# One tile's gate table summed in DRAM by accumulating indirect DMAs, its gathers given seven buffers and a higher priority

## The chip, the cores and the metric

The kernel runs on one core of a Trainium2 chip. The metric is the device time of one execution in microseconds. The kernel before took 2860.1 us (median of 3 runs, 2859.8 to 2860.92). Engines are named as in the profile: PE (matrix products), DVE, ACT and POOL (vector work), SP (issues most DMAs; indirect DMAs are issued by POOL).

## The reference, cut to what matters

One layer over 1024 rows (tokens) of width 1024: token mixing (convolutions and a gated spatial product), then a mixer called PEER, then a small gated embedding and a norm. PEER picks, for each row and each of 8 heads, 16 of 16384 experts and sums their one-neuron outputs:

```python
s1 = jnp.einsum("thd,hkd->thk", q1, sub_keys[:, 0])    # 128 scores per head and side
v1, i1 = lax.top_k(s1, TOPK)                           # the same for s2
vals, ci = lax.top_k(cand, TOPK)                       # 16 best of the 16 x 16 sums
idx = (e1 * N_KEYS + e2).reshape(t, PEER_HEADS * TOPK) # 128 picks per row
gates = jax.nn.softmax(vals, axis=-1)
ug = expert_u[ib]
act = jax.nn.gelu(jnp.einsum("td,tkd->tk", xb, ug)) * gb
vg = expert_v[ib]
return jnp.einsum("tk,tkd->td", act, vg)
```

The 16 picks of one head of a row are different experts; picks of different heads may be the same one, and then their weights add up.

## The kernel before

The 1024 rows are eight tiles of 128. PEER is done in three ways. For tiles 1 to 4 (`DENSE`) every expert is computed with matrix products against the whole of `expert_uT` and `expert_v`, and a table `Wd[t]` in DRAM (16384 experts by 128 rows, zero where nothing is picked) gives each product its gate. For tiles 5 to 7 (`GATHER`) the picked rows of `expert_u` and `expert_v` are fetched by indirect DMAs, 128 rows of 4 KB per DMA, and multiplied on DVE. Tile 0 (`MIXED`) takes one half of each: its rows of `expert_u` are gathered, which gives the 128 activations of a row times their gates (`weights[0]`, tile `wm`), and these go as values into a table `Wd[0]`, with which the dense products of `expert_v` are weighted.

The program has three stages. The **front** treats the tiles in pairs (0,1), (2,3), (4,5), (6,7): `mix_in` (projections, convolution taps on DVE), `mix_out` (output projection, norm; POOL computes the reciprocal root `rB`), `choose` (query products, the top-16 searches on DVE, `select`). A pair's `finish`, which holds its `choose`, is issued after the next pair's `mix_in`. Beside them run the gate tables: `gate_table(t)` is a generator that `fill()` advances a step at a time. It goes through the tile's 128 rows in quads of four: DVE writes a one-hot of the first key for the quad (`oh1`, L415), another engine a one-hot of the second key times the gate (`oh2`: POOL for every odd quad, L421; for even quads ACT in two steps, L426 and L427, or DVE for tile 0, L423), PE multiplies them (L430), and ACT copies the product into the tile `st` (L431). Eight quads fill `st`, which SP stores with one 2 MB DMA (L434); four such stores make a table. The gathers of tile 0 (`u_step(MIXED, ...)`, L536, and their products on DVE, L538) are written in the code after the last pair's `choose`, in four blocks of 32, each followed by a gelu on ACT (L546) and the product with the gates on POOL (L547); tile 0's table is the last of the fillers. One block of tile 5's gathers ends the front. The **dense** stage runs over the 128 blocks of experts, with the gathers of tiles 5 to 7 beside it, and then the **back** finishes all tiles.

The order in which instructions stand on each engine is set when the program is built, by a scheduler that simulates time and takes ready instructions by priority (the place in the code, unless `high_priority` moves it up). On the chip each engine runs its list in that order: an instruction that waits holds back all that stand behind it on its engine, and SP's list does the same for DMAs. So a gather that is late in the code can stand early in POOL's list. A pool with `bufs=n` gives a tile name n buffers in turn; the next writer of a buffer waits for the last reader of it. `g` (a gathered tile) has 3 buffers in the front (`FG`), `st` 2.

Of the kernel before, what the change touches and what calls it, by code (L numbers as in the profile page):

```python
# [8 lines left out]
F32 = mybir.dt.float32  # L9
# [5 lines left out]
OP = mybir.AluOpType  # L15
AX = mybir.AxisListType
P = 128
D = 1024
# [8 lines left out]
def trunk(ctx: ExitStack, tc: tile.TileContext, x, pT, w_inF, w_inV, chan, ln_c, w_sT, b_s, w_out, g_row,  # L27
# [30 lines left out]

    UAT, GAT, RATE = 6, 6, 3

    FG, BG = 3, 5

# [12 lines left out]
    TG = 32  # L75
    Wd = {t: dram.tile([P, P // TG, P, TG], F32, name=f"Wd{t}") for t in TABLE}

    fctx = ExitStack()
# [60 lines left out]
    def mix_in(t0, nt):  # L139
# [23 lines left out]
        for j in range(3):  # L163
            pg, pv = zchunks(3 + j, j)
            sg = work.tile([P, T], F32, name="sg")
            nc.scalar.activation(sg, pg, AF.Sigmoid)
            ya = work.tile([P, 30 + T], F32, name="ya", bufs=3)
            nc.scalar.copy(ya[:, 0:30], halo_a[:, j])
            nc.vector.tensor_mul(ya[:, 30:], pv, sg)
            nc.scalar.copy(halo_a[:, j], ya[:, T:T + 30])  # L170
            yas.append(ya)
        for j in range(3):
# [10 lines left out]
        for j in range(2):  # L183
# [12 lines left out]
            pb, = zchunks(6 + j)  # L196
            nc.vector.tensor_mul(yT[:, 3 + j], pb, acc)


        vn = group.tile([P, nt, 384], F32, name="vn")  # L200
        for s in range(3):
            wv = wstream.tile([P, 8, P], F32, name="w1", bufs=2)
            nc.sync.dma_start(wv, w_inV[s])
            for t in range(nt):
                pv = psum.tile([P, 2, 64], F32, name="z")
                for c in range(8):
                    nc.tensor.matmul(pv, aT[:, c, t * P:(t + 1) * P], wv[:, c], start=c == 0, stop=c == 7)
                nc.scalar.copy(vn[:, t, s * P:s * P + P], pv.rearrange("p h c -> p (h c)"))
        for t in range(nt):
            st = small.tile([P, 4, 6], F32, name="st")  # L210
# [105 lines left out]

    filler, n_gt = [], [0]

    def fill():

        for _ in range(RATE):
            while filler:
                if next(filler[0], None) is None:
                    filler.pop(0)
                    continue
                break
# [9 lines left out]
    def select(t, tv, ti):  # L336
# [27 lines left out]
        own = work if t in GATHER else wbp  # L364
        e = own.tile([P, 2, NH * K], F32, name="e", bufs=2 if t in GATHER else 5)
        for side in range(2):
# [28 lines left out]
    def gate_table(t):  # L395
# [12 lines left out]
        for g in range(P // TG):  # L408
            st = wbp.tile([P, P, TG], F32, name="st")
            for q in range(0, TG, 4):  # L410
                c = g * TG + q
                n_gt[0] += 1

                oh1 = wbp.tile([P, 4, P], F32, name="oh1", bufs=2)
# [3 lines left out]
                for k in range(4):  # L418
                    k2, gk = eT[:, 1, c + k:c + k + 1], gT[:, c + k:c + k + 1]
                    if n_gt[0] % 2:  # L420
# [11 lines left out]
                if q % 8:  # L432
                    yield True
            nc.sync.dma_start(Wd[t][:, g], st)  # L434

    def dense():
# [87 lines left out]
    def u_step(t, b, front=False):  # L524
# [9 lines left out]
        for k in range(b * KB, (b + 1) * KB):  # L534
            ug = gath.tile([P, D], F32, name="g")
            nc.gpsimd.indirect_dma_start(out=ug, out_offset=None, in_=expert_u,  # L536
                                         in_offset=bass.IndirectOffsetOnAxis(ap=idx[:, k:k + 1], axis=0))
            nc.vector.scalar_tensor_tensor(ug, ug, 1.0, ns[t, front], op0=OP.mult, op1=OP.mult,  # L538
                                           accum_out=dots[:, k - b * KB:k - b * KB + 1])
        if t == MIXED:  # L540
# [9 lines left out]
    def experts(tiles):  # L550
# [26 lines left out]
        for st in steps:  # L577
            if st not in acts:
                u_step(*st)
            if prev is not None:  # L580
# [18 lines left out]
    def back_out(t, h, nT):  # L599
# [26 lines left out]
        nc.sync.dma_start(out[t * P:(t + 1) * P], o_)  # L626

    def finish(t0, nt, nT):
# [16 lines left out]
    finish(*waits.pop())  # L645
    while filler:
        fill()
    for b in range(UE):
        u_step(GATHER[0], b, True)
    fctx.close()  # L650
# [94 lines left out]
```

## Time and profile before

| | |
|---|---|
| median of 3 runs | 2860.1 us |
| the profiled execution | 2848.63 us, span 2846.6 us |
| busy share of the span | PE 92%, DVE 76%, POOL 69%, ACT 35% |
| front: start to the first dense product (PE L481) | 0 to 1085 us |
| dense stage | to about 2620 us |
| back | to 2846.6 us |

A trace tells for each engine which instruction ran when, and which other one it waited for before. A busy share over the whole span says little here, since the three stages have different limits; the view by stretches gives the shares apart.

### The profile page before, as it was taken

Reading aid. Unit: us, or ns where it says so; the run is one execution under the profiler, and the core shown is the slowest. Engines: PE = TensorE matmul, PEld = TensorE weight load, DVE = VectorE, ACT = ScalarE, POOL = GpSimd, SP = SyncE. Lnnn points to the kernel's source line nnn. Section 1 sums busy time; section 2 is a strip of 40 time slices with the busy share of each in tenths; the row PEclk is TensorE's granted clock in tenths of the full one; section 3 lists DMA queues with packets and bytes.
Section 4 is the critical chain, followed back from the end, with each engine's and each line's share of the span. In section 5 each row is a group of like instructions: output and inputs, shape, how many; then the busy total and the mean of one; then the engine's idle time right before and its main releaser. Section 6 shows DMA issues by size and latency. Waiting matters only on the chain.

```text
span 2846.6 us, 37627 instructions
## 1 busy us (share of the span) xinstructions
PE 2607.7 (92%) x12671; PEld 2197.8 (77%) x12671; DVE 2163.0 (76%) x4738; ACT 1007.2 (35%) x1930; POOL 1951.6 (69%) x1740
## 2 busy tenths in 40 slices
PE   7999989798768568999999999999999999999988
PEld 6888878787767556888787888878788787888777
DVE  5566998899977886777777777776777777777776
ACT  3324237345655534232322223222232322222352
POOL 0000067368776787887888878887887878888783
PEclk9999999899778779999999999999999999999999
DMA  6354577787757559999999999999999999999885
GB/s 209 121 194 146 190 269 275 283 299 268 236 210 268 207 211 337 329 338 334 330 346 326 336 343 344 337 332 335 335 335 325 332 351 323 341 337 328 312 290 174
DMA packets 299697, 820.92 MB, mean 288 GB/s; under 512 B 26096, under 2 KB 117616, under 8 KB 296944
## 3 DMA queue, kind: packets, MB, share of 16 engines
q0 software_dynamic: 129024, 469.82, 45.9%
q1 hardware_dynamic: 170480, 348.70, 36.0%
q8 instruction: 100, 1.64, 0.2%
q14 instruction: 93, 0.76, 0.1%
HBM read 764.93 MB, written 53.48 MB: 288 GB/s over the span
## 4 chain that ended last, share of the span: by engine, by line
PE 43%; DVE 18%; DMA 18%; POOL 11%; issue 8%; ACT 1%; SPq 0%; POOLq 0%; DVEq 0%; ACTq 0%
DMA g<-expert_u,idx 8%; DMA g<-expert_v,idx 7%; PE mm L504 5%; PE mm L505 5%; PE mm L506 5%; PE z L481 5%; PE z L482 5%; PE z L483 5%; DVE g L538 4%; POOL g L536 3%; PE z L158 3%; PE mm L612 3%; POOL oh L421 3%; POOL vl L477 3%; PE mm L299 2%
## 5 line engine op out<-in xcount | busy, mean ns | idle before, releaser
L536 POOL DMA_INDIRECT g<-expert_u,idx x512 | 509.5, 995 | 340.1 <-DVE g L538 137.1
L568 DVE SCALAR_TENSOR_TENSOR accP<-g,act,accP 128x1024 f32<-128x1024 f32 x384 | 493.6, 1285 | 205.3 <-DMA g<-expert_v,idx 199.9
L538 DVE SCALAR_TENSOR_TENSOR g<-g,nP 128x1024 f32<-128x1024 f32 x352 | 423.2, 1215 | 168.9 <-DMA g<-expert_u,idx 167.7
L566 POOL DMA_INDIRECT g<-expert_v,idx x384 | 367.2, 956 | 143.4 <-DVE accP L568 62.0
L504 PE MATMUL mm<-vh,ah 128*128 128x512 f32 x1024 | 399.8, 392 | 16.1 <-DVE accA L508 8.8
L481 PE MATMUL z<-nh,uh 128*128 128x512 f32 x1024 | 401.5, 392 | 8.1 <-DVE al L490 5.9
L482 PE MATMUL z<-nl,uh 128*128 128x512 f32 x1024 | 400.2, 391 | 1.6 <-DVE nl L446 1.5
L483 PE MATMUL z<-nh,ul 128*128 128x512 f32 x1024 | 399.8, 390 | 0.0
L505 PE MATMUL mm<-vl,ah 128*128 128x512 f32 x1024 | 398.7, 390 | 0.0
L506 PE MATMUL mm<-vh,al 128*128 128x512 f32 x1024 | 396.4, 390 | 0.0
L421 POOL TENSOR_SCALAR oh<-iota,eT,gT 128x128 f32<-128x128 f32 x320 | 325.2, 1024 | 43.7 <-PE gt L430 39.0
L430 PE MATMUL gt<-oh,oh 128*128 128x128 f32 x1280 | 228.0, 327 | 131.6 <-DVE oh L415 69.7
L468 ACT CAST uh<-u 128x1024 fp32r<-128x1024 f32 x128 | 134.7, 1052 | 566.9 <-PE z L482 449.5
L477 POOL TENSOR_TENSOR vl<-v,vh 128x512 fp32r<-128x512 f32 x256 | 327.5, 1300 | 2.6
L430 PEld LDWEIGHTS gt<-oh,oh 128*128 128x128 f32 x1280 | 199.5, 229 | 160.7 <-POOL oh L421 92.1
L470 POOL TENSOR_TENSOR ul<-u,uh 128x1024 fp32r<-128x1024 f32 x128 | 308.7, 2412 | 3.9 <-ACT uh L468 1.9
L475 ACT CAST vh<-v 128x512 fp32r<-128x512 f32 x256 | 153.7, 621 | 319.1 <-DMA v<-expert_v 266.6
L538 DVE SCALAR_TENSOR_TENSOR g<-g,hrow 128x1024 f32<-128x1024 f32 x160 | 196.4, 1230 | 74.5 <-DMA g<-expert_u,idx 74.3
L299 PE MATMUL mm<-nT,w 128*128 128x256 f32 x1024 | 243.1, 387 | 0.0
L504 PEld LDWEIGHTS mm<-vh,ah 128*128 128x128 f32 x1024 | 193.0, 189 | 59.3 <-DVE accA L508 11.8
L508 DVE TENSOR_TENSOR accA<-mm,accA 128x512 f32<-128x512 f32 x320 | 218.1, 685 | 26.2 <-PE mm L506 25.6
L481 PEld LDWEIGHTS z<-nh,uh 128*128 128x128 f32 x1024 | 193.6, 189 | 53.0 <-DVE al L490 10.6
(367 smaller groups left out, 4593.6 us busy)
## 6 DMA issues: line engine op xcount, KB each, us to landing
u<-expert_uT SPq DMA_DIRECT2D x128, 512.0 KB, 6.1
v<-expert_v SPq DMA_DIRECT2D x128, 512.0 KB, 5.0
Wd<-st SPq DMA_DIRECT2D x20, 2048.0 KB, 8.9
w<-w_q SPq DMA_DIRECT2D x64, 512.0 KB, 4.5
w<-Wd SPq DMA_DIRECT2D x128, 256.0 KB, 10.2
w<-w_inF SPq DMA_DIRECT2D x60, 512.0 KB, 4.1
wo<-w_out SPq DMA_DIRECT2D x32, 512.0 KB, 3.4
g<-expert_u,idx POOLq DMA_INDIRECT x512, 6.2
```

Of the source, the lines that this page charges most:

```text
L421: nc.gpsimd.tensor_scalar(oh2[:, k], iota, k2, gk, op0=OP.is_equal, op1=OP.mult)
L430: nc.tensor.matmul(pw[:, :, k], oh2[:, k], oh1[:, k], start=True, stop=True)
L477: nc.gpsimd.tensor_tensor(vl, v[:, s * 512:s * 512 + 512], vh.bitcast(F32), op=OP.subtract)
L481: nc.tensor.matmul(ph, uh[:, c], nh[:, c], start=c == 0, stop=False)
L482: nc.tensor.matmul(ph, uh[:, c], nl[:, c], start=False, stop=False)
L483: nc.tensor.matmul(ph, ul[:, c], nh[:, c], start=False, stop=c == 7)
L504: nc.tensor.matmul(po, ah[:, c], vh, start=i == 0, stop=False)
L505: nc.tensor.matmul(po, ah[:, c], vl, start=False, stop=False)
L506: nc.tensor.matmul(po, al[:, c], vh, start=False, stop=i == NG - 1)
L536: nc.gpsimd.indirect_dma_start(out=ug, out_offset=None, in_=expert_u, in_offset=bass.IndirectOffsetOnAxis(ap=idx[:, k:k + 1], axis=0))
L538: nc.vector.scalar_tensor_tensor(ug, ug, 1.0, ns[t, front], op0=OP.mult, op1=OP.mult, accum_out=dots[:, k - b * KB:k - b * KB + 1])
L568: nc.vector.scalar_tensor_tensor(acc, vg, act[:, k:k + 1], acc, op0=OP.mult, op1=OP.add)
```

## The change

Tile 0's work is taken out of the chain of code that follows the last `choose`, and its table is no longer made of one-hots.

- `finish` hands tile 0, as soon as its picks are there, to a new list `slow`: the generator `mixed` runs the four blocks of gathers and then `add_table`. `fill()` advances `slow` by 14 steps (`STEP`), and is also called in `mix_in` at eight places. Each gather and its product are issued with `high_priority(offset=1000)`. `FG` goes from 3 to 7 buffers.
- `add_table` issues 128 indirect DMAs from POOL, one per pick: each adds 128 numbers of 4 bytes (the weights of pick k of the 128 rows) into `Wd[0]` at 128 computed places. The adds of one head are declared independent of each other; the head's last one waits for the other 15, and the next head's adds wait for it.
- The four parts of `Wd[0]` are first zeroed: POOL clears a tile `zero` (it is the first holder of `st`'s buffer), and SP stores it four times, 2 MB each.
- `add_places` computes the places: two DVE instructions on 128 x 128 values.
- `st` goes from 2 buffers to 1, the keys `e` of tiles 0 to 4 from 5 to 3.
- The one-hot branch on DVE (L423) goes, since only tile 0 used it. The other four tables stay as they were.

```diff
+    AHEAD, PM, PR = 1000, 2, (1,)
+    RATE, STEP = 3, 14
-    FG, BG = 3, 5
+    FG, BG = 7, 5
...
+        for _ in range(STEP):
+            turn[0] += 1
+            for w in slow[turn[0] % 2:2] + slow[:turn[0] % 2]:
+                if next(w, None) is None:
+                    slow.remove(w)
...
-            st = wbp.tile([P, P, TG], F32, name="st")
+            st = wbp.tile([P, P, TG], F32, name="st", bufs=1)
...
-                    elif t == MIXED:
-                        nc.vector.tensor_scalar(oh2[:, k], iotaP, k2, gk, op0=OP.is_equal, op1=OP.mult)
...
+    def add_table(t, at):
+        gate = weights.get(t, picks[t][1])
+        flat = Wd[t].rearrange("p g e t -> (p g e t)")[:, None]
+        last = None
+        for h in range(NH):
+            adds = []
+            for k in range(h * K, h * K + K):
+                i = nc.gpsimd.indirect_dma_start(out=flat,
+                                                 out_offset=bass.IndirectOffsetOnAxis(ap=at[:, k:k + 1], axis=0),
+                                                 in_=gate[:, k:k + 1], in_offset=None, compute_op=OP.add)
+                i = getattr(i, "ins", i)
+                if len(adds) < K - 1:
+                    for j in adds:
+                        tc.declare_no_dep(i, j, reason="picks of one head are different experts")
+                    if adds and last is not None:
+                        tc.add_manual_dep(i, last.name, SYNC, reason="picks of different heads may be the same")
+                else:
+                    for j in adds:
+                        tc.add_manual_dep(i, j.name, SYNC, reason="the head's last add ends all of them")
+                adds.append(i)
+                yield True
+            last = i
+
+    def mixed(t, at):
+        for b in range(P // KB):
+            yield from u_step(t, b, True)
+        yield from add_table(t, at)
...
+            with tc.high_priority(offset=AHEAD if t == MIXED else 0):
+                ug = gath.tile([P, D], F32, name="g")
...
+    zero = wbp.tile([P, P, TG], F32, name="st", bufs=1)
+    nc.gpsimd.memset(zero, 0.0)
+    for t in ADDED:
+        for g in range(P // TG):
+            nc.sync.dma_start(Wd[t][:, g], zero)
...
     def finish(t0, nt, nT):
         choose(t0, nt, nT)
-        if t0 == UAT:
-            for b in range(P // KB):
-                u_step(MIXED, b, True)
-        filler.extend(gate_table(t0 + t) for t in range(nt) if t0 + t in DENSE)
-        if t0 == GAT:
-            filler.append(gate_table(MIXED))
+        for t in range(t0, t0 + nt):
+            if t in ADDED:
+                slow.append((mixed if t == MIXED else add_table)(t, add_places(t)))
+            elif t in DENSE:
+                filler.append(gate_table(t))
```

The order of the instructions shows three places. The first is SP's list at the very start of the program; `w_...<-w_inF` are the weights of `mix_in`'s products, `w<-w_q` the query weights. Before:

```order
L260 DMA h<-x 128x2x1024
L263 DMA wo<-w_out 128x1024 x2
L294 DMA sk<-skT 128x256
L297 DMA w_1372<-w_q 128x1024
L297 DMA w_1382<-w_q 128x1024
L294 DMA sk<-skT 128x256
L145 DMA a<-x 128x1024 x2
L156 DMA w_227<-w_inF 128x1024
L156 DMA w_237<-w_inF 128x1024
```

and now:

```order
L268 DMA h<-x 128x2x1024
L271 DMA wo<-w_out 128x1024 x2
L693 DMA Wd_96<-st 128x4096 x4
L302 DMA sk<-skT 128x256
L305 DMA w_1383<-w_q 128x1024
L305 DMA w_1393<-w_q 128x1024
L302 DMA sk<-skT 128x256
L150 DMA a<-x 128x1024 x2
L161 DMA w_238<-w_inF 128x1024
```

The four zeroing stores stand ahead of the third weight tile of `mix_in` (`w_227`, now `w_238`) and of two query weight tiles.

The second is POOL's list around the two `rB` of the last pair (tiles 6 and 7), which `mix_out` needs before that pair's queries can start. `oh` is a quad's one-hots (four instructions), `g` a gather, `Wd_96<-wm,at` an add, `wm<-wm,gate` the end of a block of tile 0. Before:

```order
L421 TENSOR_SCALAR oh_4811<-iota,eT,gT 128x128 x4
L536 DMA g<-expert_u,idx 128x1024 x2
L421 TENSOR_SCALAR oh_5452<-iota,eT,gT 128x128 x4
L536 DMA g<-expert_u,idx 128x1024
L421 TENSOR_SCALAR oh_5482<-iota,eT,gT 128x128 x4
L536 DMA g<-expert_u,idx 128x1024 x2
L122 TENSOR_TENSOR rB<-ss_6972,half 128x1
L122 TENSOR_TENSOR rB<-ss_6991,half 128x1
L421 TENSOR_SCALAR oh_5512<-iota,eT,gT 128x128 x4
L421 TENSOR_SCALAR oh_5598<-iota,eT,gT 128x128 x4
```

and now:

```order
L602 TENSOR_TENSOR wm<-wm,gate 128x32
L467 DMA Wd_96<-wm,at 2097152x1 x15
L437 TENSOR_SCALAR oh_4869<-iota,eT,gT 128x128 x4
L467 DMA Wd_96<-wm,at 2097152x1
L437 TENSOR_SCALAR oh_4899<-iota,eT,gT 128x128 x4
L467 DMA Wd_96<-wm,at 2097152x1 x15
L437 TENSOR_SCALAR oh_4951<-iota,eT,gT 128x128 x4
L127 TENSOR_TENSOR rB<-ss_7516,half 128x1
L127 TENSOR_TENSOR rB<-ss_7535,half 128x1
L467 DMA Wd_96<-wm,at 2097152x1
L437 TENSOR_SCALAR oh_4981<-iota,eT,gT 128x128 x4
L437 TENSOR_SCALAR oh_5011<-iota,eT,gT 128x128 x4
```

Before, 118 gathers and 168 one-hots stand ahead of this pair of `rB`; now 128 gathers, 116 one-hots and 127 adds do.

The third is ACT's list in the last table (tile 0's before, tile 4's now), where `st<-gt` copies a quad's product. Before:

```order
L431 COPY st<-gt 128x128x4 x2
L371 CAST tb<-ti 128x1024
L431 COPY st<-gt 128x128x4 x2
L371 CAST tb<-ti 128x1024
L431 COPY st<-gt 128x128x4 x4
L371 CAST tb<-ti 128x1024
L431 COPY st<-gt 128x128x4 x18
L530 ACTIVATE nP<-hrow,rB 128x1024
```

and now:

```order
L439 ACTIVATE oh_7296<-iota,eT 128x128 x4
L440 ACTIVATE oh_7296<-oh_7296,gT,mT 128x128 x2
L444 COPY st<-gt 128x128x4
L440 ACTIVATE oh_7296<-oh_7296,gT,mT 128x128 x2
L444 COPY st<-gt 128x128x4
L439 ACTIVATE oh_7348<-iota,eT 128x128 x4
L440 ACTIVATE oh_7348<-oh_7348,gT,mT 128x128 x4
L439 ACTIVATE oh_7378<-iota,eT 128x128 x4
L440 ACTIVATE oh_7378<-oh_7378,gT,mT 128x128 x4
L444 COPY st<-gt 128x128x4 x4
```

Before, the copies follow one another, 18 in a row at the end; now ACT makes the one-hots of every second quad too, and between the last copy of one `st` and the first of the next (which waits for the store of the first) stand two sets of one-hots. On PE, 50 of 160 quads stand behind the last query product before, 39 of 128 now.

## Rows read from the trace of the kernel before

**Rows 1.** stretches of the kernel: busy time of each engine, granted clock, DMA share
```profile
core 0: us, PE busy (x) PEld busy (x) DVE busy (x) ACT busy (x) POOL busy (x), PEclk, DMA share, GB/s
0.00:348.00 348.00, 319.28 (x1865) 282.94 (x1866) 235.86 (x833) 111.09 (x233) 15.91 (x24) 0.99 0.50 167
348.00:547.00 199.00, 171.65 (x1084) 157.05 (x1083) 172.61 (x635) 99.42 (x240) 125.33 (x120) 0.93 0.80 280
547.00:810.00 263.00, 215.88 (x1307) 193.92 (x1306) 246.16 (x808) 143.79 (x343) 187.19 (x177) 0.90 0.76 267
810.00:944.00 134.00, 108.62 (x569) 96.01 (x569) 99.65 (x348) 71.39 (x170) 93.68 (x87) 0.85 0.63 222
944.00:1083.00 139.00, 83.28 (x399) 68.93 (x397) 113.58 (x388) 62.93 (x132) 116.34 (x119) 0.74 0.61 225
1083.00:2620.00 1537.00, 1506.53 (x6567) 1235.20 (x6568) 1129.07 (x1535) 434.70 (x676) 1263.11 (x1058) 0.99 0.95 336
```

**Rows 2.** chain that ended last, 20 to 35 us: start, length, what
```profile
20.12 3.73 PE z L158 x16
23.88 3.99 DMA w<-w_inF
27.91 7.19 PE z L158 x32
```

**Rows 3.** DVE, 348 to 810 us: its waits for gathers (total, times, longest)
```profile
DVE g L538 <- DMA g<-expert_u,idx: 43.0, 22, 6.4
```

**Rows 4.** DVE, 810 to 944 us: its waits for gathers
```profile
DVE g L538 <- DMA g<-expert_u,idx: 21.6, 7, 5.5
```

**Rows 5.** SP queue in order of time, near 11 us
```profile
10.79 0.43 SPq L294 DMA_DIRECT2D sk<-skT  x1
```

**Rows 6.** stretches between 20 and 30 us (columns as in Rows 1)
```profile
20.00:25.00 5.00, 4.88 (x23) 4.31 (x24) 0.00 (x0) 1.10 (x5) 0.00 (x0) 1.00 1.03 400
25.00:30.00 5.00, 4.39 (x21) 3.55 (x20) 0.73 (x3) 4.57 (x7) 1.00 (x2) 1.00 0.66 230
```

**Rows 7.** tile st: its four-per-table stores, from issue to landing
```profile
DMA to landing us min/median/max: 6.7/8.9/10.6
```

**Rows 8.** POOL in order of time: start, length, what, idle before
```profile
348.10 1.37 POOL L536 DMA_INDIRECT g<-expert_u,idx  x1 [16.84 <-DVE idx L392]
349.77 1.51 POOL L536 DMA_INDIRECT g<-expert_u,idx  x1 [0.30 <-issue]
357.23 0.95 POOL L536 DMA_INDIRECT g<-expert_u,idx  x1 [4.62 <-DVE g L538]
408.61 1.03 POOL L536 DMA_INDIRECT g<-expert_u,idx  x1 [0.17 <-issue]
809.50 1.77 POOL L122 TENSOR_TENSOR rB<-ss,half 128x1 f32<-128x1 f32 x2
```

**Rows 9.** POOL by line up to 1092 us: busy, mean ns, idle before
```profile
L421 POOL TENSOR_SCALAR oh<-iota,eT,gT 128x128 f32<-128x128 f32 x320 | 325.2, 1024 | 43.7 <-PE gt L430 39.0 <-ACT eT L407 1.8 <-DVE oh L377 0.6
L536 POOL DMA_INDIRECT g<-expert_u,idx x168 | 184.9, 1100 | 186.6 <-DVE g L538 87.2 <-DVE idx L392 16.8 <-DVE tv L333 13.9
```

**Rows 10.** DVE by line up to 1092 us
```profile
L538 DVE SCALAR_TENSOR_TENSOR g<-g,hrow 128x1024 f32<-128x1024 f32 x160 | 196.4, 1230 | 74.5 <-DMA g<-expert_u,idx 74.3
L415 DVE TENSOR_TENSOR oh<-iotaP,eT 128x512 f32<-128x512 f32 x160 | 106.8, 677 | 18.1 <-PE gt L430 18.1
L423 DVE TENSOR_SCALAR oh<-iotaP,eT,gT 128x128 f32<-128x128 f32 x64 | 21.9, 399 | 0.0
```

**Rows 11.** DMA issues, 348 to 810 us: the gathers, median us to landing
```profile
g<-expert_u,idx POOLq DMA_INDIRECT x118, 5.9
```

**Rows 12.** ACT by line up to 1092 us
```profile
L426 ACT ACTIVATE oh<-iota,eT 128x128 f32<-128x128 f32 x256 | 81.9, 396 | 0.0
L427 ACT ACTIVATE oh<-oh,gT,mT 128x128 f32<-128x128 f32 x256 | 107.9, 486 | 0.0
L431 ACT COPY st<-gt 128x512 f32<-128x512 f32 x160 | 91.6, 585 | 212.4 <-PE gt L430 211.7
```

More of the change, by code (lines that the diff above doesn't have):

```diff
@@ L16 @@
 AX = mybir.AxisListType
+SYNC = mybir.DependencyInfo(mybir.DependencyClass.Sync, mybir.DependencyReason.DATA)
 P = 128
@@ L76, in trunk @@
     Wd = {t: dram.tile([P, P // TG, P, TG], F32, name=f"Wd{t}") for t in TABLE}
+    ADDED = (0,)
     fctx = ExitStack()
@@ L171, in mix_in @@
             yas.append(ya)
+            fill()
         for j in range(3):
@@ L197, in mix_in @@
             nc.vector.tensor_mul(yT[:, 3 + j], pb, acc)
+            fill()
         vn = group.tile([P, nt, 384], F32, name="vn")
@@ L208, in mix_in @@
                 nc.scalar.copy(vn[:, t, s * P:s * P + P], pv.rearrange("p h c -> p (h c)"))
+            fill()
         for t in range(nt):
@@ L315, in choose @@
             picks[t0 + t] = select(t0 + t, *top[t])
-    filler, n_gt = [], [0]
+    filler, slow, turn, n_gt = [], [], [0], [0]
     def fill():
@@ L324, in fill @@
                     filler.pop(0)
+                    continue
+                break
+        for _ in range(STEP):
[3 more added lines that the diff above has]
+                    slow.remove(w)
                     continue
@@ L364, in select @@
         own = work if t in GATHER else wbp
-        e = own.tile([P, 2, NH * K], F32, name="e", bufs=2 if t in GATHER else 5)
+        e = own.tile([P, 2, NH * K], F32, name="e", bufs=2 if t in GATHER else 3)
         for side in range(2):
@@ L434, in gate_table, with add_places @@
             nc.sync.dma_start(Wd[t][:, g], st)
+    def add_places(t):
+        e = keys[t]
+        at = wbp.tile([P, NH * K], I32, name="at", bufs=3)
+        row = wbp.tile([P, NH * K], F32, name="row", bufs=1)
+        nc.vector.tensor_scalar(row, e[:, 0], float(TG), place, op0=OP.mult, op1=OP.add)
+        nc.vector.scalar_tensor_tensor(at, e[:, 1], float(P * P), row, op0=OP.mult, op1=OP.add)
+        return at
+    def add_table(t, at):
[24 more added lines that the diff above has]
+        yield from add_table(t, at)
     def dense():
@@ L534, in u_step @@
         for k in range(b * KB, (b + 1) * KB):
[L535 to L539, printed above, removed]
+            with tc.high_priority(offset=AHEAD if t == MIXED else 0):
+                ug = gath.tile([P, D], F32, name="g")
+                nc.gpsimd.indirect_dma_start(out=ug, out_offset=None, in_=expert_u,
+                                             in_offset=bass.IndirectOffsetOnAxis(ap=idx[:, k:k + 1], axis=0))
+                nc.vector.scalar_tensor_tensor(ug, ug, 1.0, ns[t, front], op0=OP.mult, op1=OP.mult,
+                                               accum_out=dots[:, k - b * KB:k - b * KB + 1])
+            yield True
         if t == MIXED:
@@ L578, in experts @@
             if st not in acts:
-                u_step(*st)
+                for _ in u_step(*st):
+                    pass
             if prev is not None:
@@ L626, in back_out @@
         nc.sync.dma_start(out[t * P:(t + 1) * P], o_)
+    place = fconst.tile([P, 1], F32, name="place")
+    for g in range(P // TG):
+        nc.gpsimd.iota(place[g * TG:g * TG + TG], pattern=[[0, 1]], base=g * P * TG, channel_multiplier=1,
+                       allow_small_or_imprecise_dtypes=True)
+    zero = wbp.tile([P, P, TG], F32, name="st", bufs=1)
+    nc.gpsimd.memset(zero, 0.0)
+    for t in ADDED:
+        for g in range(P // TG):
+            nc.sync.dma_start(Wd[t][:, g], zero)
     def finish(t0, nt, nT):
         choose(t0, nt, nT)
-        if t0 == UAT:
-            for b in range(P // KB):
-                u_step(MIXED, b, True)
-        filler.extend(gate_table(t0 + t) for t in range(nt) if t0 + t in DENSE)
-        if t0 == GAT:
-            filler.append(gate_table(MIXED))
+        for t in range(t0, t0 + nt):
[3 more added lines that the diff above has]
+                filler.append(gate_table(t))
     waits = []
@@ L645, in trunk @@
     finish(*waits.pop())
-    while filler:
+    while filler or slow:
         fill()
     for b in range(UE):
-        u_step(GATHER[0], b, True)
+        for _ in u_step(GATHER[0], b, True):
+            pass
     fctx.close()
```

3 lines of the change are left out of this document (1 added, 2 removed).

## Prediction

> **What bounds the kernel now.** I read the stretches first [rows 1]. From 1083 us on TensorE is busy 1506.5 of 1537 us, and this stage keeps its code and its order; only its start can move. So the question is when the last of the four tables lies in DRAM. Before that the limits differ by stretch. Up to 348 us it is TensorE (319.3 of 348); the chain of waits runs there through products and the weight tiles that they wait for [rows 2]. From 348 to 810, the gathers of tile 0 beside the one-hots, DVE is the fullest: 172.6 + 246.2 = 418.8 of 462 us, and the missing 43 us are its waits for gathers, 43.0 us in 22 waits [rows 3]; POOL has 125.3 + 187.2 = 312.5. From 810 to 944, with the last pair's queries, no engine is full and DVE waits 21.6 us for gathers [rows 4]. From 944 to 1083 the rest of the tables is made: POOL 116.3, DVE 113.6 of 139 us. The lists in order of time I read for what stands around POOL's gathers.
>
> **The change part by part. Zeroing.** The four stores of 128 x 4096 numbers, 8.39 MB together, stand in SP's list where `sk` is issued at 10.79 us [rows 5]; POOL's clearing of the tile has nothing ahead of it. Behind them stands the third weight tile of `mix_in`, and that tile is on the chain: it was issued at 23.88, took 3.99, and the products start at 27.91 when it lands [rows 2]. The DMA engines are full there, share 1.03 at 400 GB/s from 20 to 25 us and still 0.66 from 25 to 30 [rows 6]. With 8.39 MB put ahead, the tile lands 8.39 MB / 400 GB/s = 21 us later. TensorE is the limit up to 348 us, so this reaches the first picks: 348 becomes 369. Bounds: 0, if the weights pass beside the stores; 26.8, four times the shortest landing (6.7 us) of a store of this shape [rows 7], one after another. I take 21, which rests on the rate measured at that place.
>
> **348 to the last pair's `rB` (809.5 us, [rows 8]).** POOL gains the adds. Its list up to `rB`: 128 gathers x 1.100 = 141; 116 one-hots x 1.024 = 119 [rows 9]; other work as before, 312.5 - 118 x 1.100 - 168 x 1.024 = 11; and 127 adds. No add is in the trace of before. The nearest row is a gather, which takes as many places (128) from a column and writes other descriptors from them: 127 x 1.10 = 140. Between DMA instructions there is a pause of 0.17 to 0.30 us with nothing to wait for [rows 8]; 255 x 0.2 = 51. Sum 141 + 119 + 11 + 140 + 51 = 462 us. DVE's own list up to the same place gains 13 products and loses 24 batched one-hots: 13 x 1.23 = +16 and 24 x 0.68 = -16 [rows 10], so DVE keeps 419. For one add with its pause the low bound is 0.30 (the pause alone, the work hidden), the high one 2.5 (twice 1.10 and 0.3, as numbers are added and not only written); I take 1.30, as the undisturbed gather shows 0.95 and 1.03 + 0.17 and the mean is 1.10.
>
> The Trainium skill (DMA: Bandwidth & Descriptors, Anatomy of one DMA — SWDGE path) calls the writing of descriptors a small, variable part of such a DMA. The row says that POOL is held about 1 us by 128 of them, so here the measurement decides; by the page alone the adds would cost about their pauses, and the front would come out near case A below.
>
> POOL's 462 take the place of DVE's 419 as the limit, and waits come on top. The adds of a head wait for the head before, and the head's last add for the other 15; behind a waiting add stand the next gathers, one-hots and the `rB`, all on POOL. For most heads 8 to 10 one-hots (8 to 10 us) stand between an add and the one that waits for it; for the last two only a quad's four (4 x 1.02 = 4.1 us). A landing takes 5.9 us as a gather does [rows 11], so two waits of 1.8 = 4 us are left. Adds can't start before the first block of 32 gathers and products is done; until then POOL has 39 gathers and 24 one-hots, 39 x 1.30 + 24 x 1.02 = 75 us, and runs into DVE, which does the picks and products: I put 15 us for that, worked out from the 16.84 and 4.62 us that POOL waits for DVE around its first gathers [rows 8] with the seven buffers taking off some of it (an estimate, 0 to 30). The seven buffers hide most of DVE's 43 us; a third, 16 us, I leave as coupling of the two engines. Waits: 4 + 15 + 16 = 35. `rB` at 369 + 462 + 35 = 866 instead of 809.5.
>
> The skill's same page and section gives a fixed completion of about 2.0 us for such a DMA; the row shows 5.9 at this load. By the page the two waits at the end go, and `rB` stands 4 us earlier.
>
> **`rB` to the last query product.** 134 us before; the 21.6 us of gather waits [rows 4] end, since the gathers stand far ahead, but the table work between the queries stays; I count 12 of them: 122, so 988.
>
> **The end of the tables.** Behind the last query product 39 quads stand instead of 50, and they are tile 4's, of which ACT makes the one-hots of every second. For eight quads (one `st`) ACT has 4 sets of 4 x (81.9 + 107.9) / 256 = 2.97 us, 11.9, and 8 copies of 91.6 / 160 = 0.57, 4.6 [rows 12]: 16.4 us. `st` has one buffer now: the first copy of the next one waits until the store has landed, 8.9 us in the median [rows 7] and 0.3 to issue, of which ACT covers two sets, 5.9: 3.3 us more, 19.7. 39 / 8 x 19.7 = 96. ACT's other work there, 62.9 [rows 1] - 50 x 0.57 - 9 sets x 2.97 (tile 4's 18 quads) = 7.6, and one set of POOL's, 4.1, ahead of the first copy: 12. So 108 instead of 139. POOL has 19 or 20 quads x 4 x 1.02 = 80 there and DVE less than before (35 batched one-hots x 0.68 = 24 and the picks), neither the limit. ACT becomes it; before it mainly waited for TensorE's `gt` (211.7 us over all copies, [rows 12]).
>
> **Sum.** 866 + 122 + 108 = 1096 instead of 1083: 13 us later. The profiled execution took 2848.63 us in all with a span of 2846.6, so 2861.6. The median of the three timed runs, 2860.1, lies 11.5 above the profiled one, so the forecast is 2873 us.
>
> **Rivals.**
> A: POOL is not the limit. If an add and its pause cost 0.3 to 0.9 us, or the gathers with seven buffers keep DVE full all the time, DVE's 419 count: 369 + 419 + 18 of waits = 806, and 806 + 122 + 108 = 1036, 47 us earlier: 2813. For it: DVE waits 43.0 us for gathers now, POOL is idle for a third. Against it: 1.10 us for each gather. The point that decides: 1083 - 122 - 108 - 369 = 484 us; is POOL's work with its waits under this, the kernel is faster, above it slower. My 497 lies 13 above, and 0.1 us less for each add would do it.
> B: the adds land slowly. Each reads and writes 128 numbers of 4 bytes in DRAM, which no row shows; the nearest slow landing is the `st` store, 10.6 us at most [rows 7]. Then the last two heads wait 2 x 6.5 and the others up to 2 x 1 to 2 each: some 29 us more, 2902. At 20 us, 12 waits of 11 and three of 16 = 180: 3040. I give the far one little.
> C: the zeroing lies beside other loads, since the engines have room after 30 us: 21 us back, 2852. Against: share 1.03 just there.
> D: the change moves little. Tile 0's gathers stood from the first picks on before as well (the first at 348.10, 118 of 128 ahead of the last `rB`), so little waits went that weren't covered; table work saved and zeroing cancel: 2860.
>
> **Chances.** The forecast (POOL full, 2855 to 2905) 0.46, A with the faster half of C 0.33, B 0.12, D and what lies near it 0.09. A measurement of this kernel can tell some 0.2%, 5.7 us. Faster by more: A, and 0.03 of the forecast's and D's lower edge, 0.36. Within: 0.16, from D and the forecast's lower part. Slower: 0.48. The range takes in A's 2813 and the near case of B up to adds of 1.5 us with waits: 2810 to 2935.
>
> **What would show it.** In the profile of the changed kernel: the third `w_inF` landing near 49 us and the first gather near 369 (right), near 28 and 348 (C). POOL busy over nine tenths from 400 to 866 us and the adds' mean near 1.1 us with few waits (right); below 0.8 (A); POOL idle behind adds of landing time over 10 us (B). DVE's waits for gathers near zero; `rB` of the last pair near 866; the last query product near 988; ACT waiting for the stores of `st` some 3 us each and the last table store issued near 1096. The forecast is wrong if POOL is idle for a fourth of the stretch from 400 us on while DVE is full, or if the first products don't wait for the zeroing.

## The result and the profile after

The changed kernel takes 3009.78 us (median of four runs, 2997.45 to 3014.78) against 2860.47 us: ratio 1.0513, 95% interval 1.0485 to 1.0542, some 149 us slower. Forecast were 2873 us and a range up to 2935; the sign was right, the size was not. The profiled execution took 2997.45 us with a span of 2995.4.

The stretches of the kernel after, cut at the same events as in [rows 1]: first gather, last pair's `rB`, last query product, first dense product (columns as there).

```profile
0.00:375.00 375.00, 323.68 (x1857) 285.58 (x1858) 239.16 (x833) 111.01 (x232) 19.86 (x29) 0.95 0.51 176
375.00:976.00 601.00, 394.01 (x2199) 349.86 (x2197) 429.89 (x1461) 202.73 (x457) 506.29 (x383) 0.81 0.68 210
976.00:1114.00 138.00, 114.37 (x585) 98.31 (x585) 99.42 (x340) 75.10 (x186) 108.10 (x102) 0.86 0.65 239
1114.00:1227.00 113.00, 68.61 (x319) 59.21 (x318) 74.62 (x289) 88.60 (x216) 75.84 (x80) 0.68 0.50 181
1227.00:2765.00 1538.00, 1506.50 (x6587) 1235.27 (x6587) 1124.30 (x1526) 433.59 (x672) 1266.57 (x1058) 1.00 0.95 335
```

The three stretches in the middle for the kernel before:

```profile
348.00:811.00 463.00, 388.53 (x2393) 351.98 (x2392) 419.77 (x1445) 243.33 (x582) 313.48 (x297) 0.91 0.78 272
811.00:941.00 130.00, 105.57 (x551) 93.34 (x550) 95.65 (x337) 70.69 (x169) 89.89 (x84) 0.85 0.64 225
941.00:1085.00 144.00, 85.33 (x413) 70.61 (x411) 117.14 (x396) 65.52 (x136) 119.18 (x121) 0.75 0.61 224
```

The dense stage is as long as it was (1538 us, before 1537). In the front +27 to the first picks, +138 from there to `rB`, +8 over the queries, -31 at the end of the tables: +142. In the second stretch DVE is no longer the fullest engine (430 of 601, before 420 of 463); POOL is, 506 of 601.

POOL by line in that stretch of the kernel after (busy, mean ns, idle before and what ended it):

```profile
L467 POOL DMA_INDIRECT Wd<-wm,at x127 | 210.6, 1658 | 41.0 <-issue 34.4 <-DMA Wd<-wm,at 5.1 <-POOL wm L602 1.0
L590 POOL DMA_INDIRECT g<-expert_u,idx x128 | 149.3, 1167 | 62.0 <-issue 18.3 <-DVE idx L407 17.7 <-DVE g L592 7.8
L437 POOL TENSOR_SCALAR oh<-iota,eT,gT 128x128 f32<-128x128 f32 x116 | 141.0, 1306 | 3.0 <-PE gt L443 0.9 <-ACT eT L422 0.7
```

An add holds POOL 1.66 us in the mean and 0.32 us pass ahead of it: 252 us for 127. Only 5.1 us of that are waits for other adds to land, and they land in 3.6 us in the median. The gathers' 62.0 us include the 17.7 ahead of the first of them. POOL is busy 506.3 us and in a pause without a wait for another 34.4 + 18.3: 559 of 601 us, so its list is full.

What that does to the others is read from the waits, TensorE's of before and of after (from the first gather to `rB`; total, times, longest), and DVE's of after, which answer to [rows 3]:

```profile
PE gt L430 <- DVE oh L415: 31.5, 11, 8.5
PE gt L430 <- POOL oh L421: 13.6, 13, 3.9
```

```profile
PE gt L443 <- POOL oh L437: 163.6, 32, 26.5
```

```profile
DVE g L592 <- DMA g<-expert_u,idx: 118.0, 42, 15.9
```

The profile names the gathers' DMA as what DVE waits for, 118.0 us with seven buffers. But a gather lands in 5.6 us in the median, before in 5.9 [rows 11]; it is issued late, since it stands behind adds in POOL's list. TensorE takes its list in order, so a quad's product that waits for one-hots holds up the queries behind it. One such place, first POOL and then TensorE in order of time:

```profile
508.27 1.54 POOL L467 DMA_INDIRECT Wd<-wm,at  x1 [0.30 <-issue]
510.12 1.54 POOL L467 DMA_INDIRECT Wd<-wm,at  x1 [0.31 <-issue]
511.97 1.03 POOL L590 DMA_INDIRECT g<-expert_u,idx  x1 [0.30 <-issue]
513.30 0.96 POOL L590 DMA_INDIRECT g<-expert_u,idx  x1 [0.30 <-DMA Wd<-wm,at]
514.56 1.60 POOL L467 DMA_INDIRECT Wd<-wm,at  x1 [0.30 <-issue]
515.64 2.46 POOL L437 TENSOR_SCALAR oh<-iota,eT,gT 128x128 f32<-128x128 f32 x1
```

```profile
518.15 2.08 PE L443 MATMUL gt<-oh,oh 128*128 128x128 f32 x8 [16.51 <-POOL oh L437]
```

Fourteen adds in a row, 484.20 to 511.66, 1.54 us each for the shortest; the two gathers behind them take 1.03 and 0.96. TensorE waits 16.51 us for the one-hots behind them.

The zeroing is seen on the chain at the start, which answers to [rows 2]:

```profile
13.28 22.18 DMA Wd<-st
...
35.53 12.18 DMA w<-w_inF
...
47.75 9.56 PE z L163 x32
```

The products that began at 27.91 now begin at 47.75, and the first gather at 375.42 instead of 348.10.

### The profile page after: what moved, and what is told of

It is laid out like the page before. It is cut to its first block, busy times and chain, and to the rows that moved or that the text cites. A ratio compares the mean times of both kernels' runs of the same rounds, so it can differ in the third digit from the quotient of the medians.

```text
span 2995.4 us, 37011 instructions
## 1 busy us (share of the span) xinstructions
PE 2609.7 (87%) x12412; PEld 2192.3 (73%) x12412; DVE 2133.3 (71%) x4644; ACT 993.3 (33%) x1897; POOL 2124.5 (71%) x1809
## 4 chain that ended last, share of the span: by engine, by line
PE 40%; DMA 19%; POOL 17%; DVE 12%; issue 9%; ACT 2%; SPq 0%; POOLq 0%; DVEq 0%; ACTq 0%
DMA g<-expert_v,idx 7%; DMA g<-expert_u,idx 7%; POOL Wd L467 5%; PE mm L557 5%; PE mm L559 5%; PE mm L558 5%; PE z L534 4%; PE z L535 4%; PE z L536 4%; PE z L163 4%; POOL g L590 4%; POOL oh L437 3%; DVE g L592 3%; PE mm L307 2%; PE mm L668 2%
## 5 line engine op out<-in xcount | busy, mean ns | idle before, releaser
L590 POOL DMA_INDIRECT g<-expert_u,idx x512 | 519.2, 1014 | 200.6 <-issue 80.5
L443 PE MATMUL gt<-oh,oh 128*128 128x128 f32 x1024 | 208.3, 356 | 236.8 <-POOL oh L437 183.9
L443 PEld LDWEIGHTS gt<-oh,oh 128*128 128x128 f32 x1024 | 180.0, 253 | 266.7 <-POOL oh L437 214.1
L437 POOL TENSOR_SCALAR oh<-iota,eT,gT 128x128 f32<-128x128 f32 x256 | 277.3, 1139 | 54.4 <-PE gt L443 52.1
L592 DVE SCALAR_TENSOR_TENSOR g<-g,hrow 128x1024 f32<-128x1024 f32 x160 | 197.6, 1239 | 124.8 <-DMA g<-expert_u,idx 124.7
L163 PE MATMUL z<-aT,w 128*128 128x256 f32 x960 | 234.2, 401 | 30.3 <-DMA w<-w_inF 28.0
L467 POOL DMA_INDIRECT Wd<-wm,at x128 | 212.3, 1658 | 41.2 <-issue 34.6
```

The lines of the kernel that those rows point to most:

```text
L443: nc.tensor.matmul(pw[:, :, k], oh2[:, k], oh1[:, k], start=True, stop=True)
```

## Experiments

Theory 1: POOL's list is the limit; each add costs what it holds POOL, and the zeroing has a price of its own. Theory 2: the order counts, the runs of 15 adds ahead of one-hots, gathers and `rB`. Rivals are the adds' traffic, the new list order and the buffers. Each ratio is against the kernel before in the same batch (medians 2858 to 2865). Stretches are those of one profiled execution each; that of the kernel before took 2848.63 us, 10 to 16 less than these medians, so differences of that size between stretches prove nothing by themselves.

**e1: the zeroing alone, in the kernel before.**

```
+    zero = wbp.tile([P, P, TG], F32, name="st")
+    nc.gpsimd.memset(zero, 0.0)
+    for t in (MIXED,):
+        for g in range(P // TG):
+            nc.sync.dma_start(Wd[t][:, g], zero)
```

> The kernel before with the four zeroing stores alone, at the same place. Theory 1 (POOL full: in the changed kernel the 127 adds before the last rB hold it 210.6 us + 41.1 us of pauses ahead of them, and with 128 gathers and 116 one-hots it has no room left; the zeroing is a delay of its own): the first gather moves from 348.1 to about 375, as in the changed kernel, the rest of the front stays: 2860 + 27 = 2887 (2880 to 2893). Rival (the zeroing delays only what has slack, and all of the 142 us that the front grew by come from POOL or from the adds' traffic): 2860, within 6.

2888.48 us, ratio 1.0093 (1.0062 to 1.0123), +26. First gather at 375.36. The zeroing's price is shown, and it is not POOL's.

**e2: no adds.**

```
-            adds = []
             for k in range(h * K, h * K + K):
-                i = nc.gpsimd.indirect_dma_start(out=flat,
...
                 yield True
```

> The changed kernel with the 128 adds left out (tile 0's table stays zero, so tile 0's part of the dense stage is missing from the output); zeroing, gathers and all else stay. Theory 1: POOL's list up to the last rB shrinks from 600 to some 350 us and DVE, with 429 us busy there, is the limit again: rB at 805 to 835 instead of 974, total 2840 to 2870 instead of 3010. Rival (the list order, the run-ahead and the seven buffers hold the front back, whatever the adds cost): less than half of that, above 2940.

2833.84 us, ratio 0.9913 (0.9887 to 0.9940). So the adds cost 176 us of the 3010, and what is left of the change with its zeroing is 28 us faster than before; without the zeroing's 26 that is some 54 us, for a table less of one-hots and the earlier gathers together (no run parts the two). The time lies 6 us below the expected range, `rB` 12 us behind its own. The stretches, cut at the same events:

```profile
374.00:847.00 473.00, 388.90 (x2320) 347.65 (x2318) 433.74 (x1479) 227.44 (x531) 317.60 (x288) 0.91 0.75 272
847.00:976.00 129.00, 106.12 (x555) 92.80 (x556) 96.47 (x333) 69.72 (x171) 102.74 (x93) 0.89 0.73 267
976.00:1068.00 92.00, 49.99 (x222) 43.71 (x221) 68.19 (x277) 64.37 (x152) 57.48 (x57) 0.61 0.51 180
```

DVE is the limit again (434 of 473), and the stretch up to `rB` is no shorter than before (463): the gain lies at the end, 92 against 144, where 27 quads are left instead of 50.

**e3: writes instead of adds.**

```
-                                                 in_=gate[:, k:k + 1], in_offset=None, compute_op=OP.add)
+                                                 in_=gate[:, k:k + 1], in_offset=None)
```

> The changed kernel with each add as a plain indirect write of the same 128 numbers to the same places, with the same waits (where two picks meet, the last one stands instead of the sum). An add held POOL 1.54 us at the least, a gather 0.94. If the adding form costs the 0.6 us: writes of about 0.94, 127 x 0.6 = 76 us off, 2925 to 2945. If it is the writing of 128 numbers of 4 bytes to computed places: 1.5 still, 3000 to 3015. By the rival that the read-modify-write traffic holds up the other transfers: POOL's write stays at 1.5 but the time falls all the same, by more than 30.

2940.50 us, ratio 1.0269 (1.0232 to 1.0306): 69 us less than with adds. POOL by line, first gather to first dense product:

```profile
L467 POOL DMA_INDIRECT Wd<-wm,at x128 | 149.9, 1171 | 40.7 <-issue 35.5 <-DMA Wd<-wm,at 3.1 <-POOL wm L602 1.0
```

And the shortest, median and longest of one in ns, with adds first, then as writes:

```profile
L467 POOL DMA_INDIRECT Wd<-wm,at x128: 1538/1561/2671, 484.2 to 976.1; - x128
```

```profile
L467 POOL DMA_INDIRECT Wd<-wm,at x128: 954/994/2643, 483.7 to 915.2; - x128
```

The shortest add took 1538 ns, the shortest write 954, as a gather does. So it is the adding form, not the scatter of small numbers, that costs the 0.6 us, and 62 us off POOL's list are 69 us off the time. That it is POOL's time and not the traffic in DRAM is likely, as the writes land in 3.5 us in the median and the adds in 3.6, but not separated: the form changes both.

**e4: all one-hots on ACT.**

```
-    AHEAD, PM, PR = 1000, 2, (1,)
+    AHEAD, PM, PR = 1000, 2, ()
```

> The changed kernel with all one-hots of the tables on ACT, none on POOL (PR empty); the adds stay. Theory 1: POOL's list up to the last rB loses 141 us and stands near 455, DVE's 429 near it; rB near 850, ACT has room (160 us busy of 490 in the middle of the front, and 116 one-hots x 0.74 = 86 more); the tail, ACT bound, grows from 113 to some 39 x 4 x 0.74 + 39 x 0.57 + 16 = 153. Sum: -125 + 40 = 2925 (2895 to 2950). Rival (the adds' traffic or their waits set the time, not POOL's fullness): the middle keeps its length, and with the longer tail the time is 3010 to 3055.

2904.96 us, ratio 1.0157 (1.0130 to 1.0183): 105 us less. The total is in the expected range, its parts are not: first gather to `rB` is 554 us and not 475, and the tail 88 and not 153.

```profile
374.00:928.00 554.00, 403.15 (x2374) 365.98 (x2373) 445.41 (x1506) 352.81 (x901) 389.09 (x275) 0.85 0.75 239
1044.00:1132.00 88.00, 49.00 (x195) 40.87 (x194) 65.46 (x279) 86.25 (x221) 9.78 (x7) 0.56 0.49 179
```

No engine is full in the first of these. POOL's relief was worth much, but a full POOL is not the whole of it: up to the first dense product DVE still waits 100.7 us for gathers, which stand behind adds in POOL's list, and TensorE 79.7 us for DVE's one-hots.

**e5: half of the adds.**

```
+            if h >= NH // 2:
+                for k in range(K):
+                    yield True
+                continue
```

> The changed kernel with the adds of the first four heads alone (64 of 128; the other heads' part of tile 0's table is missing). Without any add the time was 2834, with all of them 3010: 176 us for 128. Theory 1 (POOL full from the first gathers to the last rB; DVE takes over as the limit at some 473 us, as without adds): the first 64 adds fit beside DVE's work, POOL's list is 600 - 126 = 475 us, so most of the 176 us is gone: 2860 to 2895. Rival (each add delays the program by the same amount, by its traffic or its waits): half of it, 2915 to 2930.

2922.34 us, ratio 1.0214 (1.0178 to 1.0250): 87.4 off, half of 176. The plain form of theory 1, POOL or else DVE, falls: there is no first half for free. The way to `rB` takes 555 us, with POOL busy 437 of them and DVE 440. Neither is full there: the adds delay what waits for them even where POOL has room over the stretch as a whole.

**e6 and e8b.** e6 put the zeroing later in the code, e8b did that with a quarter of the quads on POOL.

```
+        if t0 == 2:
+            zero = wbp.tile([P, P, TG], F32, name="st", bufs=1)
...
-    AHEAD, PM, PR = 1000, 2, (1,)
+    AHEAD, PM, PR = 1000, 4, (1,)
```

> The changed kernel with the zeroing put behind the first pair's queries in the code, instead of at the start, so that its stores go out between 150 and 370 us, where the DMA engines have share 0.46. If the zeroing costs its 27 us by taking the engines from the first weight tiles: third weight tile back at 28, first gather at 348, 2983 (2975 to 2990). Rival (8.4 MB cost their time wherever they stand): 3000 to 3015.

> The changed kernel with the late zeroing and with a quarter of the tables' quads on POOL and three quarters on ACT (PM 4). Theory 1: POOL's list up to the last rB loses about 70 us (58 one-hots), the front 27 by the zeroing; with all of the one-hots on ACT 105 us came off, of which ACT's and DVE's couplings took some back. -27 - 70 = 2913 (2895 to 2930). If the balance of ACT and POOL is better than with everything on ACT: under 2878 (2905 - 27).

3006.97 us (ratio 1.0508, 1.0471 to 1.0545) and 2946.81 us (1.0291, 1.0253 to 1.0329). Both are misses as experiments on the zeroing: nothing held it back, and the scheduler issued the stores at 11.23 and 10.83 us as before. So e6 is the changed kernel once more. e8b shows 63 us for half of POOL's one-hots, 105 for all of them (e4).

**e10: the zeroing held back** by a factor that comes late (a row of the tile times `rB`, and so zero).

```
+            nc.gpsimd.tensor_scalar(zero[:, 0], zero[:, 0], rB[:, 0:1], None, op0=OP.mult)
```

> The changed kernel with the zeroing truly later: POOL multiplies a row of the cleared tile by tile 0's rB, which is there at 177 us, so the four stores can't go out before; in SP's list they stand behind the third pair of x loads. (In e6 the stores had stood at 11 us as before, so that run said nothing of their place.) If the zeroing costs its 27 us by taking the engines from the first weight tiles: first gather at 348, total 2983 (2972 to 2992). Rival (8.4 MB cost their time wherever they stand): 3000 to 3015.

2995.29 us, ratio 1.0474 (1.0451 to 1.0498): 14.5 off. The first gather came at 357.28, 18 us earlier, not 27. The chain shows why: the four stores went out at 153.02 and met the next pair's weights.

```profile
149.90 6.61 PE z L163 x31
156.50 20.84 DMA w<-w_inF
```

TensorE waits 13.0 us for `w_inF` up to the first gather, in the kernel before 4.9. For 8.4 MB a place where no weight is waited for would have to be looked for; neither place was one. The list of adds changed as well (all 128 stand ahead of `rB`), and in the profile the first dense product comes 6 us earlier, not 18.

**e9: the early gathers without adds,** the table of tile 0 by one-hots at the end, no adds, no zeroing.

```
-        yield from add_table(t, at)
+        filler.append(gate_table(t))
```

> The one half of the change alone: tile 0's gathers from its picks on, with seven buffers, ahead in the lists; its table made of one-hots at the end of the other four (POOL and ACT in turn), no adds, no zeroing; five buffers of keys. If the early gathers with their buffers are worth something by themselves (DVE's 43 + 21.6 us of waits for gathers before): 2805 to 2840. Theory 1 with what the kernel without adds showed (its last rB at 847 - 27, not ahead of the 809.5 of before): no gain, 2850 to 2880.

2897.72 us, ratio 1.0128 (1.0089 to 1.0167). ACT's one-hots make negative weights zero, so tile 0's negative ones are missing in this table; the work is the same. The stretches, cut at the same events:

```profile
350.00:801.00 451.00, 365.89 (x2213) 328.47 (x2211) 422.80 (x1458) 206.92 (x473) 295.15 (x268) 0.90 0.77 279
801.00:945.00 144.00, 118.39 (x603) 102.80 (x603) 101.59 (x346) 78.30 (x193) 104.51 (x97) 0.86 0.66 239
945.00:1121.00 176.00, 116.17 (x535) 97.88 (x536) 91.24 (x316) 139.93 (x353) 118.71 (x135) 0.72 0.41 156
```

DVE's waits for gathers fall from 74.3 us (first gather to first dense product) to 26.3, but the way to `rB` is only 12 us shorter (451, before 463), about what two executions differ by. The queries take 144 instead of 130 and the tail 176 instead of 144: 65 quads are left there, not 50, and ACT instead of DVE makes every second quad's one-hots of tile 0. So the run shows no gain of the early gathers, but it isn't the gathers alone.

**e7: three gather buffers.**

```
-    FG, BG = 7, 5
+    FG, BG = 3, 5
```

> The changed kernel with three gather buffers instead of seven. DVE's waits for gathers are 124.7 us with seven; if they come from POOL's lateness (the gathers stand behind adds in its list), the buffers matter little: 3000 to 3025. If the seven buffers hide landings as the prediction had it: 3035 to 3070.

3013.11 us, ratio 1.0552 (1.0514 to 1.0590), against 3009.78: the four buffers more are worth nothing here, as expected for gathers that are late on POOL. But the scheduler's lists changed with them: 103 gathers and 79 adds stand ahead of the last `rB`, not 128 and 127.

```profile
373.00:907.00 534.00, 399.21 (x2385) 358.17 (x2383) 414.80 (x1448) 247.69 (x582) 444.11 (x358) 0.87 0.68 222
907.00:1033.00 126.00, 96.33 (x493) 84.96 (x493) 78.07 (x297) 51.56 (x129) 98.87 (x85) 0.85 0.65 206
```

`rB` comes 69 us earlier than in the kernel after, the queries end at 1033, and the first dense product still starts only at 1250.9, with POOL busy 183 of the 218 us between. Up to there DVE waits 166.9 us for gathers instead of 124.7. So the equal time doesn't show that landings cost nothing with three buffers. It shows an earlier `rB` that gained nothing: the work on POOL was put off, not taken away.

**e11: at most three adds behind each of POOL's quads.**

```
+                if adder and n_gt[0] % PM in PR:
+                    for _ in range(3):
+                        next(adder[0], None)
...
+                tc.add_manual_dep(i, quad[0].name, SYNC, reason="an add behind each quad")
```

> The changed kernel with the same adds, one-hots and zeroing, but at most three adds issued behind each of POOL's quads (each add is made to wait for the quad before it), where now 15 of one head follow one another between two quads. 60 adds then stand before the last rB instead of 127, the rest between the later quads. Theory 2 (the runs: while POOL issues 15 adds, 15 x 1.9 us, TensorE, in order, waits for the next one-hots, with all that stands behind, 163.6 us of such waits from 348 to 975 us against 24.4 before): 2910 to 2950. Theory 1 in its plain form (POOL's sum is the limit, 690 us busy and some 75 us of pauses from 375 to 1227, whatever the order): 2980 to 3015. If only what stands ahead of the last rB counts: 67 adds less there, about 3010 - 67 x 1.4 = 2915, but the tail longer by the same 67 adds where POOL is busy 76 of 113 us, so 2950 to 2980.

2980.08 us, ratio 1.0428 (1.0400 to 1.0456): 30 off, the edge of what theory 1 expected and far from theory 2's 60 to 100. The stretches show what happened:

```profile
373.00:904.00 531.00, 414.59 (x2329) 366.13 (x2328) 442.20 (x1486) 233.22 (x540) 411.90 (x349) 0.85 0.73 246
904.00:1040.00 136.00, 99.81 (x480) 86.84 (x479) 87.97 (x319) 49.67 (x119) 115.55 (x97) 0.85 0.69 224
1040.00:1200.00 160.00, 69.71 (x293) 58.00 (x292) 71.67 (x285) 82.44 (x197) 139.80 (x121) 0.60 0.44 117
```

`rB` comes 70 us earlier, as 60 adds stand ahead of it and not 127. The other 68 come later, and the tail grows from 113 to 160 us with POOL the fullest in it (140 of 160). Up to the first dense product TensorE still waits 173.4 us for POOL's one-hots, in 82 pieces; in the changed kernel it was 183.9 in 56. The waits moved with the order of the adds, as theory 2 had it, but their total stayed, as theory 1 had it.

**e12, e13, e14: mends together.** All have the late zeroing and adds spread behind the quads of both engines; e12 a quarter of the one-hots on POOL and two adds for a quad, e13 none on POOL and two adds, e14 none and one add.

> Three mends together: the late zeroing of e10, a quarter of the quads' one-hots on POOL and three quarters on ACT (as e8b, whose zeroing stood early), and two adds behind each quad (of both engines). From 3010: -27 for the zeroing, -63 for POOL's share (e8b gave 2947), and of the waits for one-hots behind runs of adds most of the rest. If the parts add up: 2830 to 2880, about the kernel before (2862) or a little faster. If ACT is late instead (in e4 its one-hots waited on casts and tables): 2880 to 2930.

> Late zeroing, all one-hots on ACT, and two adds behind each quad instead of runs of 15. With ACT's one-hots and the runs (e4) POOL was busy only 428 of 759 us and the front still 64 us longer than without adds; DVE waited 100.7 us for gathers, up to 15.3 at once, as gathers stand behind runs of 13 to 15 adds in POOL's list. Theory 2 in this form (the runs ahead of gathers and rB): those waits fall below 50, total 2835 to 2875. Theory 1 alone (each add costs its 1.96 us wherever it stands): 2905 - 15 for the zeroing = 2890 (2880 to 2905).

> As e13 with one add behind each quad: 29 adds stand ahead of the last rB instead of 58, and more behind the last query product. Theory 2: rB and the last query product another 20 to 40 us earlier than in e13, the tail longer by the adds that are left (POOL has nothing else there): 2830 to 2880. Theory 1 alone: 2880 to 2905.

2935.51 us (ratio 1.0265, 1.0242 to 1.0288), 2907.13 (1.0179, 1.0147 to 1.0211) and 2945.09 (1.0313, 1.0280 to 1.0346). None is faster than the kernel before, and all three lie above every range that was expected for them, by 2 to 40 us: the parts didn't add up. e13, its three stretches:

```profile
357.00:836.00 479.00, 384.02 (x2271) 341.95 (x2270) 430.34 (x1481) 293.96 (x737) 259.92 (x198) 0.89 0.77 266
836.00:966.00 130.00, 95.52 (x514) 84.77 (x513) 87.81 (x301) 89.30 (x235) 98.02 (x70) 0.89 0.78 247
966.00:1128.00 162.00, 93.54 (x350) 77.42 (x351) 87.57 (x328) 149.71 (x401) 63.76 (x42) 0.56 0.43 132
```

DVE's waits for gathers fell below 50 as theory 2 had it (45.8), and `rB` came 92 us earlier than in e4, 17 of them by the first gather; then the tail grew from 88 to 162 us with ACT full (149.7), and 43 quads were left for it instead of 24. The total is e4's. In e14 the first dense product starts at 1089.8, 5 us behind the kernel before's 1085.00; but the last add is issued at 1193.68. From 1085 to 1260 us TensorE waits for POOL's part of the dense stage, which stands between the adds (total, times, longest):

```profile
PE z L544 <- POOL ul L531: 42.5, 2, 21.3
```

In e12 the way to `rB` is 504 us, 97 less than in the kernel after, but the queries take 156 and the tail 143, 18 and 30 more. In each of the three a part of what was taken off one place came back at a later one.

## Why the prediction was wrong

The forecast lay 136 us low for the profiled execution (2861.6 against 2997.45). By its own steps:

- **Zeroing:** 21 us, measured 27.3 (375.42 - 348.10), and 26 alone in e1. Right in its mechanism, just past its upper bound of 26.8. The third weight tile landed 20 us later, and the 32 products behind it took 9.56 us instead of 7.19: TensorE had waited 19.5 us, and its mean granted clock from 30 to 50 us was 0.55, before 1.00. Where the other 5 us arose was not followed. Rival C is refuted.
- **First gather to `rB`:** 462 + 35 = 497, measured 599 (375.42 to 974.25). This is the step that failed, and in it one term, the price of an add. The prediction took the nearest row, a gather with a pause: 1.30 us, 127 x 1.30 = 165. Measured are 210.6 + 41.0 = 252 us in all; less the 5.1 of landings, which had a term of their own, 1.94 us for one: 82 of the 102 us. The value lies inside the bounds that were given, 0.30 to 2.5. With 1.94 put in, the same sum would have given `rB` at 954 with the zeroing as measured (measured 974), so POOL as the new limit of this kernel was right. That the longer of two lists, POOL's or DVE's, sets the time at any number of adds is not: half of the adds still cost half (e5). The range of the end left the bounds of the add out: 127 x (2.5 - 1.30) = 152 us more would have been 3025, and the forecast range stopped at adds of 1.5.
- **One-hots on POOL:** 119, measured 141.0 with 3.0 of idle. Here 25 us are missing. Some one-hots begin before the add ahead of them ends (the 515.64 above), but the lines' busy times sum to 511.1 and POOL is busy 506.3, so at most 5 are overlap; the other 20 are one-hots that took longer, 1.22 us each instead of 1.02. Why is open.
- **Waits on POOL:** 4 us for landings; measured 5.1, right. Gathers with pauses and waits 211 (149.3 + 62.0) less the 17.7 ahead of the first, 194; the prediction had 141 + 26 and 31 of coupling, 198. Rival B, slow landings, came near in its second figure (3040; its own sum, 2873 + 180, makes 3053), but by luck: an add lands in 3.6 us, faster than a gather. The sign that DVE's waits for gathers would be near zero failed, with 118.0 us: seven buffers don't help a gather that POOL issues late.
- **Queries:** 122, measured 138. It was expected that of DVE's 21.6 us of waits for gathers 12 would come back. The waits did fall, to 6.7 us, but the time did not: TensorE waits 16.9 us for POOL's one-hots there (before 6.8 for POOL's and 16.6 for DVE's), and POOL has tile 5's 32 gathers beside them (108 of 138 us busy).
- **End of the tables:** 108, measured 113.7 (1113.8 to 1227.5), and ACT is the fullest engine there (88.6 of 113) as said. ACT's wait for `st`'s store is 2.9 us there, in one piece and not five times 3.3.
- **Rival A** gave too much: even without any add (e2) the time is 2833.84, 28 us below the kernel before and not 47. Its deciding point, 484 us from the first gather to `rB`, was passed by 115 (599).

On rival D: a run with the early gathers and no adds shows no gain (e9), one with fewer buffers no loss (e7), but in both the lists or the engine of some one-hots changed too.

The Trainium skill (DMA: Bandwidth & Descriptors, Anatomy of one DMA — SWDGE (gpsimd) path) calls the writing of descriptors a small, variable part of a DMA. In these traces POOL is held at least 1.54 us by an add of 128 places and 0.95 by a plain write of them (e3), which is not small against landings of 3.6 and 3.5 us; how much of the hold is the writing, no run shows.

**What stays open.** Why an accumulating indirect DMA holds POOL 0.6 us longer than a plain one is not seen in the profile. And of the 176 us that the adds cost, the runs don't say how much is POOL's sum and how much is delay handed from engine to engine. By count the cost is even: the first 64 adds cost 89 us (e5 against e2) and the second 64 cost 87, for 131 and 122 us of POOL's time. Shortening each add is worth more for each us: 62 off POOL's list by e3 gave 69. Why is not shown.

## What to carry to other kernels

When work moves to an in-order engine, price its instructions by their own form: an accumulating indirect DMA is not a gather, and where no row shows it, let the range of the end carry the whole bound of its price times its count. Look at what the moved instructions are queued with: here they stood ahead of one-hots, gathers and `rB`, all on POOL, so other engines waited while POOL had room elsewhere in the front. And follow a gain through to the last stage before believing it; spreading the adds moved `rB` by 70 us (e11) and 92 (e13 against e4), and the end by 30 or not at all.

## What the runs showed of the hardware

- An accumulating indirect DMA of 128 rows of 4 bytes held POOL 1.54 us at the least, the same DMA without the addition 0.95 (e3), a gather of 128 rows of 4 KB 0.94; so here POOL's time went by the form, not by the bytes.
- The landing of an add took 3.6 us in the median, that of a gather, with a thousand times the bytes, 5.6 in the same stretch; a plain write of the same numbers took 3.5 (e3).
- TensorE's mean granted clock from the first gather to `rB` was 0.81 after and 0.91 before (1 is 2.4 GHz, the lower level is 1.2): TensorE was busy 394 us with 2199 matmuls, before 389 with 2393. Its waits for POOL's one-hots came to 163.6 us there, the longest 26.5; before they came to 13.6, with 31.5 for DVE's. Without the adds (e2) the clock was 0.91 again, with 15.4 us of such waits for POOL.
